# An encoder block on one core: operands, merges, outputs and gates of the attention in pinned pieces, another order at the start of the MLP, the rotary angles later

## The chip, the core and the metric

One core of a Trainium2 chip. The engines that matter: PE (TensorE, the matmuls; PEld are its weight loads), DVE (VectorE), ACT (ScalarE), POOL (GpSimd) and SP (SyncE, which here only issues DMAs). Each runs its own instructions strictly in order and waits for semaphores of the others. The metric is the device time of one execution, in microseconds; "before" is the median of three.

## The reference, cut to what matters

```python
a = rms_norm(h, g_mix[i])
qa, ka, va, qd, kd, vd, gate_na, gate_dil = jnp.split(a @ w_in[i], split_points, axis=-1)
y_na = merge(neighborhood_attention(heads(qa, NA_HEADS), ..., rpb[i]))          # 8 heads of 64
y_dil = merge(dilated_attention(rotary(heads(qd, DIL_HEADS), positions),         # 3 groups x 4 heads,
                                rotary(heads(kd, DIL_HEADS), positions), ...))   # merged by softmax sums
mixed = (jax.nn.sigmoid(gate_na) * (y_na @ w_branch_na[i])
         + jax.nn.sigmoid(gate_dil) * (y_dil @ w_branch_dil[i]))
h = h + mixed @ w_out[i]
c = rms_norm(h, g_mlp[i])
h = h + jnp.square(jax.nn.relu(c @ w_up[i])) @ w_down[i]                         # 1024 -> 4096 -> 1024
e = rms_norm(h, g_ple[i])
h = h + jax.nn.sigmoid(e @ w_ple_gate[i]) * (p[i] @ w_ple_proj[i])
return rms_norm(h, g_final)
```

1024 tokens, 1024 features, one layer, float32 throughout.

## The kernel before

Every float32 operand is split into a high part (a cast, on ACT, line 109) and a low part (the difference, on DVE or POOL, line 110), and each product is three matmuls: high x high, low x high, high x low (lines 208 to 210). So PE needs three passes, and ACT and DVE have a split to make for every operand.

The stages, in us of the profiled execution: v projections (`v_unit`, PSUM tile `ps_v`) and the first RMSNorm to 155; the q and k projections to 375; 12 dilated heads to about 540; 8 NA heads to about 712; the two branch products with the gates (`ps_b`) to 798; `w_out` with the second norm (`ps_t`) to 886; the MLP up (`pp`) to 1205, the MLP down (`ps_d`) to 1510, each by a seven-product scheme on 2 x 2 blocks (b11, b21, b22, t1 to t4, where the t are sums of blocks, made on POOL and DVE); then the input embedding's gate and the final norm.

A scheduler lays out the instructions of each engine from a model of their costs; what is inside `keep_in_program_order` stays, on its engine, in the order of the program. All of a tile's softmax is pinned.

*Attention.* One loop over tiles (128 queries of one head); each step issues the scores of the tile three ahead, the transposes of the present one, its value product two steps later, and matmuls of the gate projection as fill (`pay`). A list `after` holds functions for after a given step, and `later(n, f)` puts f there n steps on. A NA tile: PE scores (`sc`), DVE adds the bias and takes the maximum (`s_sb`, L644, L646), ACT exponential (L647), DVE reciprocal (`rs`, L721), POOL scales (L722), PE transposes (`tp_p`, L731), ACT and DVE split (`pt_h`, `pt_l`), PE values (`av`). The next head's operands (`operands`, L613 to L628) are q scaled and its low half (`q_st`, ACT whole, DVE 64 x 1024) and k and its low part (`k_st`, ACT; `k_lo`, DVE for the NA heads, POOL for the dilated). `dil_merge` and `dil_out` (L937 to L968) weigh the three dilated groups together, each group a whole 128 x 1024 multiply and add (`nm_d`, `fb_d`, `y_d`) on DVE, in the NA heads. Their outputs (`y_raw`, `y_op`) are split after the last head, and the gates (`gt`) are loaded and put through the sigmoid inside the branch loop, at a place that the scheduler chooses.

*Start of the MLP.* `fast_head(u)` loads the first half of block u of `w_up` (`f_raw`) and splits b11 and b21, `fast_sums` loads the second half (`f_raw2`) and makes t1 and t2 on POOL (`f_t`). `norm_to_ops` normalizes a row of tokens, transposes it and makes the sums of the left operand (`s2`, `s3`, `s4`, `keep`). Both share buffers with the `w_out` weights (`ring`, tag `w_raw`).

Of the kernel before, what the change touches and what calls it, by code (L numbers as in the profile page):

```python
# [59 lines left out]
def encoder_kernel(ctx: ExitStack, tc: tile.TileContext, t: dict, out: bass.AP):  # L60
# [236 lines left out]
    with ExitStack() as st:  # L297
# [41 lines left out]

        pi = qp.tile([P, 256], I32, name="pi", tag="rt")  # L340
        for a in range(4):
            nc.sync.dma_start(pi[a * 32:(a + 1) * 32],
                              t["positions"][:, a * 256:(a + 1) * 256].broadcast_to((32, 256)))
        invf = qp.tile([P, 1], F32, name="invf", bufs=1)
        nc.sync.dma_start(invf, t["invf"])
        hpi = qp.tile([P, 1], F32, name="hpi", bufs=1)
        nc.vector.memset(hpi, float(np.pi / 2))
        r, k1, k2, ab, sn, cn = (qp.tile([P, 256], F32, name=n_, tag="rt") for n_ in "abcdef")
        nc.vector.tensor_copy(r, pi)
        nc.vector.tensor_scalar(r, r, invf, None, op0=ALU.mult)  # L350
        big = 4096.0 * TWO_PI
        nc.vector.tensor_scalar(k1, r, 1.0 / big, MAGIC, op0=ALU.mult, op1=ALU.add)
        nc.vector.tensor_scalar(k1, k1, MAGIC, None, op0=ALU.subtract)
        cp = _fixed_parts(big, [2.0 ** (8 - 7 * i) for i in range(8)])
        pp = _fixed_parts(TWO_PI, [2.0 ** (-9 - 12 * i) for i in range(3)])

        def less(k, part, dst=r):
            nc.vector.scalar_tensor_tensor(dst, k, -part, r, op0=ALU.mult, op1=ALU.add)

        for i in range(3):  # L360
            less(k1, cp[i])
        less(k1, cp[3], k2)
        nc.vector.tensor_scalar(k2, k2, 1.0 / TWO_PI, MAGIC, op0=ALU.mult, op1=ALU.add)
        nc.vector.tensor_scalar(k2, k2, MAGIC, None, op0=ALU.subtract)
        less(k2, pp[0])
        less(k1, cp[3])
        less(k2, pp[1])
        less(k1, cp[4])
        less(k1, cp[5])
        less(k2, pp[2])  # L370
        less(k1, cp[6])
        less(k1, cp[7])
        lim = float(np.nextafter(np.float32(np.pi), np.float32(0)))
# [1181 lines left out]
```

## Time and profile before

| what | value |
|---|---|
| median of three executions | 1651.51 us (1649.92 to 1652.97) |
| profiled execution | 1654.93 us, of which the span 1653.1 us |
| mean granted clock of PE | 0.979 |
| PE busy | 1561.5 us, 94% of the span |
| DVE busy | 1193.6 us, 72% |
| ACT, POOL busy | 708.4 us (43%), 652.6 us (39%) |

The span is the time from the first to the last instruction. A clock of 1.00 is 2.4 GHz and a clock of 0.5 is 1.2 GHz, at which each matmul takes twice as long; a mean between them says for what share of a stretch PE ran slow.

### The profile page before, as it was taken

The numbers are of one execution on the slowest core, as the hardware profiler recorded it, in microseconds if no ns is written. First come the engines' busy times: TensorE is split into PE (matmuls) and PEld (weight loads), VectorE is DVE, ScalarE is ACT, GpSimd is POOL, SyncE is SP. The second block draws the span as 40 slices with busy tenths as digits, with TensorE's granted clock in tenths as the row PEclk, the third lists the DMA queues.
The fourth block names the chain that finished last, engine by engine and source line by source line (L and its number), as shares of the span: only waits on it lengthen the run. The fifth ranks groups of instructions, "written<-read, shape, count | busy, mean of one in ns | idle before, by whom it ended". The sixth has DMA issues, their size and how long they took to land. (4 is left out here: it accounts for less than half of the span.)

```text
span 1653.1 us, 22585 instructions
## 1 busy us (share of the span) xinstructions
PE 1561.5 (94%) x7787; PEld 1308.2 (79%) x7787; DVE 1193.6 (72%) x2081; ACT 708.4 (43%) x1327; POOL 652.6 (39%) x434
## 2 busy tenths in 40 slices
PE   8899999999999998889997899999989999999997
PEld 6899777787888877667786688888867788887886
DVE  6744799734666877655458777777778999999855
ACT  7322222226888755654234333333345333323422
POOL 0233578613333222234214677777733322325100
PEclk9999999999999999999998899999999999999999
DMA  8552455675676777655343344444467444434122
GB/s 295 175 152 102 126 167 162 202 259 204 207 215 225 237 240 241 182 179 162 127 166 115 115 140 147 141 147 149 162 234 267 156 163 143 153 102 139 35 101 71
DMA packets 114482, 277.12 MB, mean 168 GB/s; under 512 B 14176, under 2 KB 30528, under 8 KB 113856
## 3 DMA queue, kind: packets, MB, share of 16 engines
q1 hardware_dynamic: 108608, 265.19, 48.9%
q10 hardware_dynamic: 5760, 10.49, 1.7%
q8 instruction: 62, 1.02, 0.2%
q14 instruction: 52, 0.43, 0.1%
HBM read 185.57 MB, written 90.06 MB: 167 GB/s over the span
## 5 line engine op out<-in xcount | busy, mean ns | idle before, releaser
L109 ACT CAST w_hi<-w_raw 128x512 fp32r<-128x512 f32 (+2 forms) x103 | 83.7, 826 | 137.9 <-POOL w_raw L470 56.0
L110 POOL TENSOR_TENSOR w_lo<-w_raw,w_hi 128x512 fp32r<-128x512 f32 (+2 forms) x33 | 64.3, 1951 | 162.0 <-ACT w_hi L109 117.6
L110 DVE TENSOR_TENSOR f_lo<-f_raw,f_hi 128x512 fp32r<-128x512 f32 x80 | 81.6, 1037 | 49.2 <-ACT f_hi L109 48.6
L110 DVE TENSOR_TENSOR w_lo<-w_raw,w_hi 128x1024 fp32r<-128x1024 f32 (+1 forms) x70 | 84.2, 1209 | 36.1 <-ACT w_hi L109 35.8
L722 POOL TENSOR_SCALAR s_sb<-s_sb,rs 128x384 f32<-128x384 f32 x64 | 40.0, 626 | 136.6 <-DVE rs L721 69.1
L110 DVE TENSOR_TENSOR pt_l<-tp_p,pt_h 128x384 fp32r<-128x384 f32 (+3 forms) x120 | 65.1, 542 | 27.0 <-ACT pt_h L109 25.6
L109 ACT CAST f_hi<-f_raw 128x512 fp32r<-128x512 f32 x80 | 46.2, 614 | 79.8 <-DMA f_raw<-w_up 75.7
L109 ACT CAST pt_h<-tp_p 128x384 fp32r<-128x384 f32 (+3 forms) x120 | 56.2, 469 | 33.5 <-PE tp_p L731 27.2
L1178 POOL TENSOR_TENSOR u_t<-u_t 128x512 f32<-128x512 f32 x45 | 53.2, 1183 | 39.9 <-ACT u_t L1177 38.7
L1177 ACT ACTIVATE u_t<-u_t 128x512 f32<-128x512 f32 x45 | 28.4, 631 | 74.5 <-DVE u_t L1164 74.1
L628 POOL TENSOR_TENSOR k_lo<-k_lo,k_st 128x1024 fp32r<-128x1024 f32 x12 | 32.1, 2678 | 65.0 <-ACT k_st L625 47.0
L1341 DVE TENSOR_TENSOR h<-ps_d,h 128x512 f32<-128x512 f32 x84 | 54.7, 681 | 2.4 <-PE ps_d L210 2.2
L110 DVE TENSOR_TENSOR f_lo<-f_t,f_hi 128x512 fp32r<-128x512 f32 x32 | 51.3, 1608 | 1.8
L637 PE MATMUL sc<-k_st,q_st 128*128 128x384 f32 (+3 forms) x160 | 52.3, 327 | 0.2 <-DVE stats L655 0.2
L638 PE MATMUL sc<-k_lo,q_st 128*128 128x384 f32 (+3 forms) x160 | 49.1, 307 | 2.7 <-POOL k_lo L628 2.7
L657 ACT ACTIVATE s_sb<-s_sb,stats 128x256 f32<-128x256 f32 (+2 forms) x96 | 44.9, 469 | 14.9 <-DVE stats L655 14.4
L731 PE MATMUL tp_p<-ident,s_sb 128*128 128x128 f32 x192 | 33.9, 288 | 17.1 <-POOL s_sb L722 15.1
L647 ACT ACTIVATE s_sb<-s_sb,nm 128x384 f32<-128x384 f32 x64 | 39.5, 617 | 23.8 <-DVE nm L646 19.6
L1341 DVE TENSOR_TENSOR sum_t<-ps_d,sum_t 128x512 f32<-128x512 f32 x72 | 46.8, 682 | 2.9 <-PE ps_d L210 2.9
L731 PEld LDWEIGHTS tp_p<-ident,s_sb 128*128 128x128 f32 x192 | 25.1, 147 | 29.9 <-POOL s_sb L722 20.4
L210 PE MATMUL ps_d<-w_hi,m_op 128*128 128x512 f32 x112 | 44.3, 405 | 2.6 <-DVE m_op L110 2.6
L644 DVE CUSTOM_DVE_ANT_0 s_sb<-bias,sc 128x384 f32<-128x384 f32 x64 | 35.1, 548 | 15.8 <-PE sc L638 14.1
(482 smaller groups left out, 5809.1 us busy)
## 6 DMA issues: line engine op xcount, KB each, us to landing
f_raw<-w_up SPq DMA_DIRECT2D x32, 512.0 KB
w_raw<-w_in SPq DMA_DIRECT2D x26, 512.0 KB
u_raw<-l_scr SPq DMA_DIRECT2D x25, 512.0 KB
qk_scr<-o SPq DMA_DIRECT2D x96, 128.0 KB
h<-l_scr SPq DMA_DIRECT2D x24, 512.0 KB
l_scr<-u_t SPq DMA_DIRECT2D x42, 256.0 KB
l_scr<-u_s SPq DMA_DIRECT2D x42, 256.0 KB
w_raw<-w_qk SPq DMA_DIRECT2D x20, 512.0 KB
```

Of the source, the lines that this page charges most:

```text
L109: nc.scalar.copy(hi, src)
L110: eng.tensor_tensor(lo, src, hi.bitcast(F32), op=ALU.subtract)
L210: nc.tensor.matmul(ps, sl, mh, start=False, stop=last)
L637: pe(nc.tensor.matmul(o, qs[:, qsl], kk, start=True, stop=False))
L638: pe(nc.tensor.matmul(o, qs[:, qsl], ll, start=False, stop=True))
L644: nc.vector.tensor_tensor_reduce(s_[:, :n], bias, sc[:, :n], 1.0, -3.0e38, op0=ALU.subtract, op1=ALU.max, accum_out=mx)
L647: nc.scalar.activation(s_[:, :n], s_[:, :n], AF.Exp, bias=nm, scale=1.0, accum_out=sm)
L657: nc.scalar.activation(s_[:, :n], s_[:, :n], AF.Exp, bias=nm, scale=-1.0, accum_out=sm)
L722: nc.gpsimd.tensor_scalar(pr, pr, rs, 1.0, op0=ALU.mult, op1=ALU.mult)
L731: pe(nc.tensor.transpose(tp[:, i * P:(i + 1) * P], pr[:, kb * P:(kb + 1) * P], ident))
L1178: nc.gpsimd.tensor_tensor(c, c, c, op=ALU.mult)
L1341: nc.vector.tensor_tensor(d, ps, d, op=ALU.add)
```

## The change

Eight edits, none of which changes what is computed or the number of matmuls:

1. The rotary angles (24 DVE operations, two sines on ACT, their DMAs) move from before the v products to after the second v unit.
2. `operands(h)` returns four steps, spread with `later` over four tiles: q's low half in two 64 x 512 pieces and, for NA heads, k's low part in two 128 x 512 pieces, all pinned; for NA heads from the fourth tile after the raw load, for dilated heads from the third tile of the head before.
3. `dil_merge` runs after NA tile 6, `dil_out` after 22 and 38, and its multiplies and adds are halves, 3, 4 and 5 tiles after the loads instead of 5 and 6.
4. Outputs 4 and 5 are split inside the last NA head, the other four after it, all in pinned halves.
5. The gates are loaded and put through the sigmoid in program order, three ahead of their use.
6. `w_out` ends with the half rows (6,0), (7,0), (6,1), (7,1); the heads of MLP blocks 0 and 1 come before (6,1); the norms of rows 6 and 7 follow with high priority; the last row's `keep` and block 0's second half use spare `ring` tiles; the first four MLP products are b11 of blocks 0 and 1, then b21 of both.
7. The first chunk of the MLP down runs b11, b21, b22, t1 ... instead of the order in `DOWN`; the second half of the last chunk's `u_scr` loads into a free operand tile (`u_more`) after b11 of that chunk.
8. The last tile's gate product is cut 384 + 128 instead of 256 + 256 columns.

```diff
         s1 = []
         for u in range(5):
             v_unit(u)
+            if u == 1:
+                angles()
...
+            def q_low(c):
+                keep(nc.vector.scalar_tensor_tensor(qs[b, c], q_raw[b, c], -0.125, qs[b, c].bitcast(F32),
+                                                    op0=ALU.mult, op1=ALU.subtract))
+            def step_0():
+                keep(nc.scalar.activation(qs, q_raw, AF.Copy, scale=-0.125))
+                q_low(cols[0])
+            def step_1():
+                keep(nc.scalar.copy(ks, kf))
+                q_low(cols[1])
...
-            if cb == 2 and qt == 1 and h < 7:
-                ready_ops.append(operands(h + 1))
             if qt == 0:
                 na_loads(*((h, cb + 1) if cb < 3 else (h + 1, 0)))
+            elif cb == 0 and h < 7:
+                load_raw(h + 1)
+                for n, f in enumerate(operands(h + 1)):
+                    later(3 + n, f)
...
-            later(5, scaled)
-            later(6, added)
+            later(3, lambda: scaled(0))
+            later(4, lambda: (scaled(1), added(0)))
+            later(5, lambda: added(1))
...
+        for n, f in ((50, lambda: y_load(4, "bias", 3)), (53, lambda: y_split(4, "kl", 3)), (54, lambda: y_load(0, "md", 2)),
+                     (55, lambda: y_load(1, "md", 2)), (56, lambda: y_split(5, "st", 4)), (57, lambda: y_load(2, "bias", 3))):
+            after.setdefault(na_0 + n, []).append(f)
...
+            load_row(NT - 1)
+            half_row(NT - 1, 0)
+            heads = [fast_head(u) for u in range(2)]
...
+            half_row(NT - 2, 1)
+            with tc.high_priority(offset=150):
+                norm_to_ops(np_, op_, *before.pop())
+                half_row(NT - 1, 1)
+                norm_to_ops(np_, op_, *before.pop())
+            late = fast_sums(0, heads[0], spare[1], op_.tile([P, D], F32, name="f_t", tag="keep"))
...
+                if u == 0:
+                    p1[0], p1[1] = head_1(0), head_1(1)
+                    for v in range(2):
+                        head_2(v, p1[v])
                 fast_rest(heads[u], *late)
...
+        first_order = ("b11", "b21", "b22", "t1", "t2", "t3", "t4")
...
+                if o == "b11":
+                    u_more = m_ops[0].bitcast(F32).rearrange("p (f n) -> p f n", f=2)
+                    nc.sync.dma_start(u_more, u_scr[2:4].rearrange("f p n -> p f n"))
```

How the order of the engines moves, at three places. DVE in an NA head, where the next head's operands meet the second `fb_d` of a dilated output; before:

```order
L964 TENSOR_TENSOR fb_d<-nm_d,fb_d 128x1024
L721 RECIPROCAL rs<-sm 128x1
L110 TENSOR_TENSOR pt_l<-tp_p,pt_h 128x3x128
L644 ISA s_sb,mx<-bias,sc 128x384
L644 ISA mx 128x1
L627 SCALAR_TENSOR_TENSOR q_st<-q_raw,q_st 64x1024
L644 ISA s_sb,mx<-bias,sc 128x384
L644 ISA mx 128x1
L628 TENSOR_TENSOR k_lo<-k_lo,k_st 128x1024
L110 TENSOR_TENSOR pt_l<-tp_p,pt_h 128x3x128
L646 TENSOR_SCALAR nm<-mx 128x1
L968 TENSOR_TENSOR y_d<-y_d,fb_d 128x1024
```

and of the change, the same operands and the first half of the same `fb_d`:

```order
L633 SCALAR_TENSOR_TENSOR q_st<-q_raw,q_st 64x512 x2
L674 TENSOR_SCALAR nm<-mx 128x1
L637 TENSOR_TENSOR k_lo<-k_lo,k_st 128x512
L110 TENSOR_TENSOR pt_l<-tp_p,pt_h 128x3x128
L749 RECIPROCAL rs<-sm 128x1
L110 TENSOR_TENSOR pt_l<-tp_p,pt_h 128x3x128
L672 ISA s_sb,mx<-bias,sc 128x384
L672 ISA mx 128x1
L749 RECIPROCAL rs<-sm 128x1
L674 TENSOR_SCALAR nm<-mx 128x1
L637 TENSOR_TENSOR k_lo<-k_lo,k_st 128x512
L1003 TENSOR_TENSOR fb_d<-nm_d,fb_d 128x512
```

Four whole operations stood within twelve rows; now the pieces are halves with the softmax of other tiles between them.

ACT at the end of the last NA head, before (`gt` is the sigmoid of a gate, `s_sb` a tile's exponential):

```order
L1058 ACT_TABLE_LOAD
L1058 ACTIVATE gt<-gt 128x1024
L109 CAST pt_h<-tp_p 128x3x128
L647 ACT_TABLE_LOAD
L647 ACTIVATE s_sb,sm<-s_sb,nm 128x384
L762 COPY fold<-av 64x512
```

and of the change, after the last tile:

```order
L1073 CAST y_op<-y_raw 128x512 x6
L1073 CAST y_op<-y_na 128x512 x2
L1110 ACT_TABLE_LOAD
L1110 ACTIVATE gt<-gt 128x1024 x4
```

Sigmoids no longer stand between the exponentials, and there is one table load where there were five.

POOL at the start of the MLP, before (`f_raw_9112` is block 0's second half, `f_raw_9379` block 1's; `keep` and `s4l` with `s_9172` are row 7's sums):

```order
L186 TENSOR_TENSOR f_t<-f_raw_9112,f_raw 128x512
L186 TENSOR_TENSOR f_t<-f_raw_9379,f_raw 128x512
L187 TENSOR_TENSOR f_t<-f_raw_9112,f_t 128x512
L188 TENSOR_TENSOR f_raw_9112<-f_raw_9112 128x512
L187 TENSOR_TENSOR f_t<-f_raw_9379,f_t 128x512
L188 TENSOR_TENSOR f_raw_9379<-f_raw_9379 128x512
L189 TENSOR_TENSOR f_raw<-f_raw,f_t 128x512 x2
L1118 TENSOR_TENSOR keep<-keep,s_9172 128x512
```

and of the change (`f_raw_9428` is block 1's second half, `w_lo` block 0's, `keep` and `w_hi` the sums of rows 6 and 7, `s4l` a low part of each):

```order
L189 TENSOR_TENSOR f_raw<-f_raw,f_t 128x512
L1184 TENSOR_TENSOR keep<-keep,s_9138 128x512
L1185 TENSOR_TENSOR keep<-keep,hx 128x512
L110 TENSOR_TENSOR s4l<-keep,s4h 128x512
L1184 TENSOR_TENSOR w_hi<-w_hi,s_9209 128x512
L1185 TENSOR_TENSOR w_hi<-w_hi,hx 128x512
L186 TENSOR_TENSOR f_t<-w_lo,f_raw 128x512
L110 TENSOR_TENSOR s4l<-w_hi,s4h 128x512
```

Block 0's first sum (t1) stood ahead of the last row's sums; now it stands behind five operations for rows 6 and 7.

## Rows read from the trace of the kernel before

**Rows 1.** The page, its first part: busy time of each engine with its share of the span and its instructions.

```profile
PE 1561.5 (94%) x7787; PEld 1308.2 (79%) x7787; DVE 1193.6 (72%) x2081; ACT 708.4 (43%) x1327; POOL 652.6 (39%) x434
```

**Rows 2.** Stretches of the run (from:to in us): length, then busy time (and instructions) of PE, PEld, DVE, ACT and POOL, the granted clock of PE as a share of full speed, the DMA share and GB/s.

```profile
50.00:75.00 25.00, 19.64 (x141) 18.97 (x140) 16.93 (x42) 7.10 (x11) 2.61 (x2) 0.86 0.41 113
75.00:150.00 75.00, 75.00 (x628) 75.00 (x627) 40.42 (x46) 20.21 (x32) 31.36 (x19) 1.00 0.50 155
...
375.00:575.00 200.00, 194.33 (x1186) 164.87 (x1185) 132.66 (x411) 159.14 (x400) 63.01 (x40) 1.00 0.66 213
575.00:700.00 125.00, 108.46 (x601) 92.59 (x600) 90.71 (x261) 75.09 (x166) 28.44 (x43) 0.92 0.72 226
700.00:725.00 25.00, 19.72 (x98) 14.89 (x96) 14.87 (x21) 17.77 (x23) 5.59 (x5) 1.00 0.63 194
725.00:800.00 75.00, 69.82 (x296) 56.41 (x297) 39.27 (x52) 31.99 (x40) 34.66 (x22) 0.98 0.49 156
...
875.00:950.00 75.00, 57.40 (x227) 45.00 (x226) 60.55 (x78) 30.37 (x57) 44.95 (x31) 0.86 0.34 113
...
1200.00:1300.00 100.00, 91.46 (x373) 72.03 (x372) 82.56 (x84) 47.51 (x58) 36.09 (x15) 0.95 0.63 227
...
1475.00:1525.00 50.00, 46.20 (x200) 37.53 (x199) 48.17 (x71) 13.49 (x24) 30.70 (x18) 0.97 0.30 105
```

**Rows 3.** From 30 to 70 us: the first transposes of PE after its longest stop there (start, length, operation, idle time before with its releaser); the angles' line 358 (length, DVE busy and instructions, clock, DMA share, GB/s); another of their lines as a group (count, busy us, mean ns, idle before).

```profile
58.94 1.12 PE L275 MATMUL tp<-ident,xn 128*128 128x128 f32 x4 [5.31 <-DVE act10l L110]
...
30.00:70.00 40.00, 4.96 (x12) 0.91 0.52 162
...
L349 DVE CAST a<-pi 128x256 f32<-128x256 int32 x1 | 0.3, 295 | 1.0 <-DMA pi<-positions 1.0
```

**Rows 4.** What PE waited for from 375 to 575 us: line, releaser, us in total, times, longest.

```profile
PE sc L638 <- POOL k_lo L628: 2.7, 3, 1.2
```

**Rows 5.** What PE waited for from 575 to 700 us (the same columns); then in order of time one of these stops: DVE from 640 to 648 us and PE at its end.

```profile
PE tp_p L731 <- POOL s_sb L722: 14.6, 6, 4.4
...
640.03 2.02 DVE L964 TENSOR_TENSOR fb_d<-nm_d,fb_d 128x1024 f32<-128x1024 f32 x1
...
643.07 1.22 DVE L627 SCALAR_TENSOR_TENSOR q_st<-q_raw,q_st 64x1024 fp32r<-64x1024 f32 x1
...
644.80 1.22 DVE L628 TENSOR_TENSOR k_lo<-k_lo,k_st 128x1024 fp32r<-128x1024 f32 x1
...
646.47 1.21 DVE L968 TENSOR_TENSOR y_d<-y_d,fb_d 128x1024 f32<-128x1024 f32 x1
...
649.56 0.90 PE L731 MATMUL tp_p<-ident,s_sb 128*128 128x128 f32 x3 [4.35 <-POOL s_sb L722]
```

**Rows 6.** Loads of the NA stretch: the issue of a `q_raw` on SP and its first use on ACT, and the issue of the two `fb_d` whose first use is the DVE row at 640.03 above. No use has an idle mark, so none waited.

```profile
561.57 0.33 SPq L613 DMA_DIRECT2D q_raw<-qk_scr  x1
...
574.83 1.07 ACT L624 ACTIVATE q_st<-q_raw 128x1024 fp32r<-128x1024 f32 x1
...
628.98 1.14 SPq L960 DMA_DIRECT2D fb_d<-f_scr  x2
```

**Rows 7.** What PE waited for from 700 to 725 and from 725 to 800 us, and one of ACT's five table loads in the last NA head.

```profile
PE ps_b L208 <- ACT y_op L109: 1.5, 1, 1.5
...
PE ps_b L208 <- DVE gt L1064: 3.0, 2, 1.8
...
700.38 1.28 ACT L1058 ACT_TABLE_LOAD   x1
```

**Rows 8.** The start of the MLP: two of w_out's matmuls on PE (24 starts apart), what PE waited for from 875 to 950 us, SP's load of the first w_up block, and rows of DVE and POOL.

```profile
879.67 0.39 PE L210 MATMUL ps_t<-w_hi,act11l 128*128 128x512 f32 x1
...
885.11 0.39 PE L210 MATMUL ps_t<-w_hi,act11l 128*128 128x512 f32 x1
...
PE pp L208 <- ACT f_hi L109: 8.2, 1, 8.2
PE pp L208 <- ACT act10h L109: 5.0, 1, 5.0
...
884.80 0.33 SPq L183 DMA_DIRECT2D f_raw<-w_up  x1
...
907.39 5.15 DVE L110 TENSOR_TENSOR f_lo<-f_t,f_hi 128x512 fp32r<-128x512 f32 x3
...
914.87 0.68 DVE L110 TENSOR_TENSOR f_lo<-f_raw,f_hi 128x512 fp32r<-128x512 f32 x1
...
908.57 3.42 POOL L189 TENSOR_TENSOR f_raw<-f_raw,f_t 128x512 f32<-128x512 f32 x2
918.32 1.28 POOL L1118 TENSOR_TENSOR keep<-keep,s 128x512 f32<-128x512 f32 x1 [6.33 <-DVE s L1115]
919.56 1.73 POOL L1119 TENSOR_TENSOR keep<-keep,xn 128x512 f32<-128x512 f32 x1
```

**Rows 9.** What PE waited for from 1200 to 1300 us.

```profile
PE ps_d L210 <- DVE m_op L110: 2.6, 1, 2.6
```

**Rows 10.** Around 1500 us: SP's second load into u_raw, one of DVE's four splits of it, and PE.

```profile
1488.24 0.38 SPq L1380 DMA_DIRECT2D u_raw<-u_scr  x1
...
1496.85 1.77 DVE L110 TENSOR_TENSOR act00l<-u_raw,act00h 128x512 fp32r<-128x512 f32 x1
...
1504.42 0.47 PE L208 MATMUL ps_d<-w_hi,act00h 128*128 128x512 f32 x1 [3.48 <-DVE h L1341]
```

More of the change, by code (lines that the diff above doesn't have):

```diff
@@ L337, in encoder_kernel @@
             norm_to_act(qp, two(xs[tt]), g, tt, xn=qp.tile([P, D], F32, name="xn", tag="nat"))
[L340 to L373, printed above, removed]
-        nc.vector.tensor_scalar(r, r, lim, -lim, op0=ALU.min, op1=ALU.max)
-        nc.vector.scalar_tensor_tensor(ab, r, -1.0, r, op0=ALU.mult, op1=ALU.max)
-        nc.scalar.activation(sn, r, AF.Sin)
-        nc.scalar.activation(cn, ab, AF.Sin, bias=hpi, scale=-1.0)
-        for i, src in enumerate((cn, sn)):
-            nc.sync.dma_start(cs_scr[i].rearrange("a f n -> (a f) n"), src)
         def v_unit(u):
@@ L833, in dil_score @@
                     dil_v(g_, pr_, pair, 0)
+            if qi == 2:
+                for n, f in enumerate(operands(h + 1 if h < 19 else 0)):
+                    later(1 + n, f)
             if qi == 4:
-                ready_ops.append(operands(h + 1 if h < 19 else 0))
                 if h < 19:
@@ L999, in encoder_kernel @@
         nc.sync.dma_start(blk, t["blk"])
-        ready_ops.append(operands(8))
+        for f in operands(8):
+            f()
         early[0] = True
@@ L1128, in encoder_kernel, with half_row @@
             w8 = take(8, 0)
-            before = None
-            for tt in range(NT):
+            sums, before = {}, []
+            def half_row(tt, n):
+                hx, parts = sums[tt]
+                ps = tok_product(w8, tt, n)
+                c = slice(n * HALF, (n + 1) * HALF)
+                nc.vector.tensor_tensor(hx[:, c], ps, hx[:, c], op=ALU.add)
+                parts.append(square_part(np_, hx[:, c], ps))
+                if n == 1:
+                    nc.sync.dma_start(h_scr[tt * P:(tt + 1) * P, :], hx)
+                    before.append((hx, g, tt, parts))
@@ L1131, in encoder_kernel, with load_row @@
+            def load_row(tt):
                 hx = op_.tile([P, D], F32, name="hx", tag="hx", bufs=2)
                 nc.sync.dma_start(hx, t["x"][tt * P:(tt + 1) * P, :])
-                parts = []
+                sums[tt] = (hx, [])
+            for tt in range(NT - 2):
+                load_row(tt)
                 for n in range(2):
-                    ps = tok_product(w8, tt, n)
-                    c = slice(n * HALF, (n + 1) * HALF)
-                    nc.vector.tensor_tensor(hx[:, c], ps, hx[:, c], op=ALU.add)
-                    parts.append(square_part(np_, hx[:, c], ps))
-                    if before is not None and n == 0:
-                        norm_to_ops(np_, op_, *before)
-                    if tt == NT - 1 and n == 0:
-                        heads = [fast_head(u) for u in range(2)]
-                        late = fast_sums(0, heads[0], op_.tile([P, D], F32, name="f_raw2", tag="hx", bufs=2),
-                                         op_.tile([P, D], F32, name="f_t", tag="keep"))
@@ L1282, in encoder_kernel @@
         ops, lefts, raws = {}, {}, {}
+        first_order = ("b11", "b21", "b22", "t1", "t2", "t3", "t4")
+        seq = [(0, o) for o in first_order] + [(c, o) for c in range(1, 7) for o in DOWN]
         def load_left(n):
@@ L1351, in encoder_kernel @@
                 load_left(n)
-            for o in DOWN:
+            for o in first_order:
                 operands(0, o)
```

185 lines of the change are left out of this document (130 added, 55 removed).

## The prediction

> **What bounds the kernel now.** I read the page's busy times first. PE is busy 1561.5 of 1653.1 us [rows 1], the other engines far less, and the change leaves PE's matmuls as many as they were. So it can only give back time in which PE stood or ran below full speed. The second view cuts the run into stretches [rows 2]. In each, the loss is (length − PE busy) + (1 − clock) × length; the second term is right because at the lower level, 1.2 GHz, half of the time is lost, and the mean clock falls by the same half. This gives for 50–75 us 5.4 + 3.5 = 8.9; 375–575 (dilated heads) 5.7; 575–700 (NA heads) 16.5 + 10.0 = 26.5; 700–725 5.3; 725–800 (branch products) 5.2 + 1.5 = 6.7; 875–950 (start of the MLP) 17.6 + 10.5 = 28.1; 1200–1300 (start of the MLP down) 8.5 + 5.0 = 13.5; 1475–1525 3.8 + 1.5 = 5.3. Together 100 us: that is all that these edits can reach. The third view is what PE waited for in each stretch, and the fourth the rows just ahead of such a stop.
>
> **The change part by part.**
>
> *Angles.* From 30 to 70 us DVE spends 4.96 us on line 358 [rows 3] and about 2.4 on eight more operations of their kind, of which the cast of 0.30 us is one; 7.4 us in all, between the norms whose transposes PE waits for. PE's longest stop there is 5.31 us, for DVE's split of a transposed tile [rows 3], and the slow clock after it costs 3.5. At the new place, after the second v unit, DVE is busy 40 of 75 us and PE never stands [rows 2], so the operations are covered; without that cover they would cost their 7.4. Nothing needs the tables before q and k. Bounds 0 and −8.9; most of the 7.4 us stands ahead of the stop, so I take −7.
>
> *Dilated operands.* PE waits 2.7 us for `k_lo` from POOL [rows 4]; the rest of the 5.7 is spread thin. The operands start two tiles earlier, which covers `k_lo`. Bounds 0 and −5.7; I take −3.
>
> *NA operands, merge and dilated outputs.* PE waits 14.6 us, in six stops, for POOL's scaled probabilities [rows 5], though POOL is busy 28 of 125 us. The rows ahead of the stop of 4.35 us show why: from 640 to 648 us DVE runs 2.02 + 1.22 + 1.22 + 1.21 = 5.7 us of other work, and the maxima and reciprocals that POOL needs are queued behind it. That work comes to halves, a tile apart, so no more than about 1.3 us (two halves) should stand together where 2 did, and the operands no longer fall on the outputs' `y_d`. But the work itself stays: DVE is busy 90.7 us here, and eight output pieces come in, each about 0.68 us [rows 8], 5.4 in all: 96. Were the whole loss to go, 98.5 us would be left and DVE 98% full, which an engine that works in order beside two others will not reach. With 12 us back it is 96 of 113, 85%, about what stretches without stops bear. Bounds −4 (one long stop goes) and −22; I take −12.
>
> *Outputs and gates.* After the last tile PE waits for `y_op`, and later for `gt` [rows 7]; these two stretches lose 12.0. Two of six outputs are ready by then. Sigmoids no longer stand between exponentials: five ACT table loads of 1.28 us [rows 7] become one, 5.1 us less on ACT in the last head. Gates loaded three ahead take away ACT's waits for them. The first branch product still has to wait for four outputs split in a row. Bounds −3 and −11; I take −8.
>
> *Start of the MLP.* The `w_up` load leaves SP at 884.80 [rows 8] and the last product of `w_out` ends at 885.5, so PE waits 8.2 us for the cast of it, then 5.0 for transposed tokens. Now the heads load before the last half rows, so the first stop shrinks to an estimated 1.5 us. Four products follow, 48 matmuls at (885.11 − 879.67)/24 = 0.227 us [rows 8], 10.9 us. Then t1 is wanted. Its first sum now stands in POOL's queue behind five operations for rows 6 and 7, each 1.28 to 1.73 us [rows 8], 7.5 in all; these start when row 7's sums leave DVE, by my estimate 10 us after the end of `w_out` (the transposes, two copies, three adds). So t1 comes 10 + 7.5 + 1.3 + a cast and a split of 1.3 = 20 us after, and PE has run dry at 1.5 + 10.9 = 12.4: a new stop of 7 to 9 us. Of the 17.6 us of standing about 11 remain, and of the slow clock its share, 11/17.6 × 10.5 = 6.5, and 1.5 for the rest: 19 of 28.1. I take −9; bounds +5 (the queue of loads on SP is late too) and −20 (the sums keep up).
>
> The row that speaks against this part: three DVE splits took 5.15 us, 1.7 each, while POOL ran its own sums (3.42 us for two), and 0.68 us once POOL had stopped [rows 8]. The Trainium skill (GPSIMD Engine Reference, section 8, Key points) says that POOL shares its SBUF interfaces with DVE and contends with DVE instructions that have two SBUF inputs; the trace agrees, with 1.7 against 0.68 us. By that rule the six DVE operations ahead of t1 would take 6 us longer and the term would be −3.
>
> *MLP down.* The stop of 2.6 us for the low part of `m_op` [rows 9] and those after it come from operands made by DVE out of the last up blocks; the new order asks for the same cast and load in its third product. I take 0; bounds +4 and −4.
>
> *Second half of `u_scr`.* Its load leaves SP at 1488.24, and its splits fall among DVE's last evacuations, one at 1496.85 taking 1.77 us; PE then stops 3.48 us at 1504 for DVE's `h` [rows 10]. Loaded early, the splits stand among the earlier sums. Bounds 0 and −5.3; I take −4.
>
> *Last tile.* The same columns in two other pieces: 0, ± 0.5.
>
> Sum: −7 − 3 − 12 − 8 − 9 + 0 − 4 = −43. The profiled execution took 1654.93 us, 1.8 more than its span and 3.4 more than the median; from it 1611.9, from the median 1651.51 − 43 = 1608.5.
>
> **The rivals.**
>
> *DVE is the bound of the NA heads.* The clumps are smaller, but the work is the same plus 5.4, and two `y_na` folds, a q half and a `y_d` half can still stand in a row. For it: DVE is over 80% busy wherever PE stops long. Against: 575–700 has 34 us of idle DVE. Then NA gives nothing and the outputs 4 instead of 8: 43 − 16 = 27, 1624.5.
>
> *The start of the MLP keeps its loss,* as t1 comes later by POOL and the port: term 0, 43 − 9 = 34, 1617.5.
>
> *Slower: pinned operations wait for their loads.* ACT's scaling of q is now pinned three tiles after its load, and each dilated output's multiply three tiles instead of five after `fb_d`. A tile takes (712 − 540)/64 = 2.7 us, three 8.1. Before, 13.3 us lay between the load and the cast of `q_raw`, and 11.0 for `fb_d` [rows 6], so landings after 8.1 us would not have shown. Seven casts and six multiplies stand ahead of the softmax in their queues. If the loads take all that time, the waits are 7 × 5.2 + 6 × 2.9 = 54 us, and 1651.5 − 43 + 54 = 1662; it decides from 43/13 = 3.3 us each, landings at 11.4 us. Against: the 1 MB of a head's q and k needs 4.6 us at the 226 GB/s of this stretch [rows 2].
>
> *No effect:* the stops come back elsewhere as the next tile's, within 3 us of 1651.5.
>
> **How the numbers follow.** Chances: forecast 0.57 (its own range 1599 to 1617), DVE bound 0.17, MLP start 0.13, no effect 0.05, slower 0.08. The predicted time is 1608.5. Below, the bounds of NA and MLP start together (−10, −11) would reach 1588, but hardly both: 1593. Above, both first rivals at once give 1633.5, which I take as 1634. A measurement of this kernel tells about 0.2%, 3.3 us, from no change. Faster 0.87, same 0.05, slower 0.08.
>
> **What would show it.** Right: in 50–75 us PE's stop for DVE under 1 us; in the NA heads stops for POOL's `s_sb` under 8 us together; one table load after the last head; at the start of the MLP one long stop, before t1, with POOL's sums as its cause; no stop at 1504. Wrong: ACT or DVE idle for `q_raw` or `fb_d` in the heads; DVE over 95% busy there with PE still stopping; a first MLP stop as long as before.

## The result and the profile after

The changed kernel takes **1623.33 us** (median of four, 1622.1 to 1625.92) against 1652.24 for the kernel before beside it; the ratio is 0.9825 with a 95% interval of 0.9807 to 0.9843, so 26 to 32 us less. The forecast was 1608.5, in a range of 1593 to 1634: faster as forecast, by 29 us instead of 43. The profiled execution took 1623.57 us, its span 1621.8.

The first part of the page after, to be read beside [rows 1]:

```profile
PE 1544.0 (95%) x7787; PEld 1294.8 (80%) x7787; DVE 1200.7 (74%) x2125; ACT 700.8 (43%) x1329; POOL 658.0 (41%) x434
```

The same stretches as in [rows 2] (length, busy time of PE, PEld, DVE, ACT and POOL, granted clock, DMA share, GB/s). Stages come 8 us earlier at 375 us and 31 at the end, so the stretches hold somewhat later work than before.

```profile
50.00:75.00 25.00, 24.47 (x207) 24.27 (x206) 19.64 (x26) 8.62 (x14) 10.55 (x7) 1.00 0.73 211
375.00:575.00 200.00, 193.38 (x1198) 165.21 (x1197) 142.13 (x458) 159.15 (x407) 59.53 (x43) 1.00 0.67 214
575.00:700.00 125.00, 114.40 (x656) 96.16 (x655) 98.01 (x278) 81.22 (x177) 37.62 (x44) 0.99 0.77 251
875.00:950.00 75.00, 63.05 (x264) 50.66 (x265) 57.85 (x64) 29.49 (x53) 54.95 (x38) 0.91 0.31 102
1200.00:1300.00 100.00, 93.35 (x397) 75.79 (x396) 97.83 (x95) 48.16 (x55) 33.92 (x12) 0.97 0.65 224
```

PE's waits after (line, releaser, us in total, times, longest), from 50 to 75, 375 to 575, 540 to 700, 685 to 800, 840 to 950, 1185 to 1300 and 1450 to 1500 us, a "..." between two stretches:

```profile
PE tp L275 <- DVE ny L248: 0.5, 1, 0.5
...
PE tp_p L890 <- DVE pt_l L110: 2.8, 3, 1.4
...
PE tp_p L759 <- POOL s_sb L750: 6.3, 8, 1.4
PE tp_p L759 <- DVE pt_l L110: 2.4, 2, 1.3
...
PE ps_b L208 <- DVE gt L1127: 3.9, 3, 1.6
PE ps_b L208 <- ACT y_op L1073: 2.3, 1, 2.3
...
PE pp L208 <- ACT f_hi L109: 12.2, 2, 11.0
...
PE ps_d L210 <- DVE m_op L110: 4.6, 2, 3.4
PE ps_d L208 <- ACT act11h L109: 3.6, 1, 3.6
...
PE ps_d L208 <- DVE sum_t L1436: 1.5, 2, 1.1
PE ps_d L208 <- DVE h L1436: 1.0, 1, 1.0
```

What the reader is to see: the 5.31 us stop at 59 us is gone; the stops for `s_sb` are no fewer than before, but short; at the start of the MLP one stop of 11 us stands in the place of two of 8 and 5; and in the place of the stop of 3.48 us at 1504 there are three of 0.3 to 1.1 us.

To compare stages that have moved I counted, for each, the time between starts of PE's matmuls beyond the usual time of their form (it holds stops and slow clock together); this is what a stage "lost". To 75 us it fell from 13.9 to 5.8; in the q and k projections it was 8.8 and 9.3; from the first score to the first branch product 43.4 and 23.7; in the branch products 10.1 and 9.4; from there to the first MLP product 10.2 and 1.8; in the next 168 matmuls of the MLP up 17.4 and 19.8; in the rest of the MLP up **−0.1 and 6.9**; in the first 84 matmuls of the MLP down 11.2 and 13.2, in the others 10.1 and 4.0. Together −31 us, as the two spans say. The 6.9 us in the middle of the MLP up are what the prediction did not have at all.

The changed kernel starts its branch products ahead of the last tile's value products, so the attention is best read between matmuls that both kernels have in the same number. From the first score to the first value product of the NA heads it takes 154.0 us before and 153.2 after; from there to the value products of the last six tiles 164.7 and 148.9; and from there to the first matmul of `w_out` 90.3 and 86.5. The second of these stretches, before and after:

```profile
537.82:702.48 164.66, 147.75 (x837) 126.61 (x837) 121.66 (x362) 104.07 (x230) 38.25 (x59) 0.94 0.71 224
...
528.79:677.68 148.89, 140.00 (x836) 119.56 (x836) 127.27 (x390) 99.80 (x230) 44.70 (x60) 1.00 0.80 256
```

### The profile page after: what moved, and what is told of

Read it like the earlier page. It is cut to its first block, busy times and chain, and to the rows that moved or that the text cites. A ratio compares the mean times of both kernels' runs of the same rounds, so it can differ in the third digit from the quotient of the medians.

```text
span 1621.8 us, 22641 instructions
## 1 busy us (share of the span) xinstructions
PE 1544.0 (95%) x7787; PEld 1294.8 (80%) x7787; DVE 1200.7 (74%) x2125; ACT 700.8 (43%) x1329; POOL 658.0 (41%) x434
## 5 line engine op out<-in xcount | busy, mean ns | idle before, releaser
L750 POOL TENSOR_SCALAR s_sb<-s_sb,rs 128x384 f32<-128x384 f32 x64 | 46.3, 724 | 112.6 <-DVE rs L749 65.3
L109 ACT CAST pt_h<-tp_p 128x384 fp32r<-128x384 f32 (+3 forms) x120 | 55.7, 468 | 26.2 <-PE tp_p L759 21.3
L685 ACT ACTIVATE s_sb<-s_sb,stats 128x256 f32<-128x256 f32 (+2 forms) x96 | 44.9, 469 | 14.8 <-DVE stats L683 13.9
L210 PE MATMUL ps_d<-w_hi,m_op 128*128 128x512 f32 x112 | 42.9, 391 | 4.6 <-DVE m_op L110 4.6
L499 POOL TENSOR_TENSOR o<-x,c 128x512 f32<-128x512 f32 x24 | 40.6, 1707 | 11.2 <-DVE c L494 8.7
L208 PE MATMUL ps_b<-y_op,w_hi 128*128 128x512 f32 x96 | 38.3, 401 | 6.3 <-DVE gt L1127 3.9
L208 PE MATMUL ps_d<-w_hi,m_op 128*128 128x512 f32 x112 | 43.6, 390 | 0.0
```

The costliest lines, as they stand in the source:

```text
L109: nc.scalar.copy(hi, src)
L208: nc.tensor.matmul(ps, sh, mh, start=first, stop=False)
L210: nc.tensor.matmul(ps, sl, mh, start=False, stop=last)
L499: nc.gpsimd.tensor_tensor(dst, x, y, op=op)
L685: nc.scalar.activation(s_[:, :n], s_[:, :n], AF.Exp, bias=nm, scale=-1.0, accum_out=sm)
L750: nc.gpsimd.tensor_scalar(pr, pr, rs, 1.0, op0=ALU.mult, op1=ALU.mult)
```

## The experiments

All times are medians beside runs of the kernel before on the same chip; what counts is the ratio to these. In us of 1651.5, the changed kernel has −28.9.

### Each part alone

The first three put one group of edits into the kernel before, the fourth takes one out of the changed kernel.

`e1_angles`, edit 1 alone:

```diff
+            if u == 1:
+                angles()
```

> The kernel before with edit 1 alone (the angles after the second v unit). Theory: the stop of 5.31 us before the transposes at 59 us and the slow clock behind it go, the rest of the run is as before: 1651.5 - 8 = about 1644 (the first 75 us lost 13.9 us before and 5.8 us in the changed kernel). Rival: the time won is given back at the next shared limit, within 3 us of 1651.5.

Measured 1644.49 us, ratio 0.9945 (0.9928 to 0.9962): −9.1. The first 75 us lost 5.8 as in the changed kernel, and nothing was given back. The forecast's −7 had the right place and was 2 short by the median, though inside the interval (−6.3 to −11.9); the first theory holds.

`e2_attention`, edits 2 to 5 alone:

```diff
+                for n, f in enumerate(operands(h + 1)):
+                    later(3 + n, f)
...
+            later(3, lambda: scaled(0))
...
+        for k, tag, bufs in ((0, "v_t", 3), (1, "st", 4), (2, "pt_h", 2), (3, "pt_l", 2)):
+            y_split(k, tag, bufs)
...
+        for n in range(3):
+            gate_in(n)
```

> The kernel before with edits 2 to 5 alone (operands, merge, outputs, gates). By the two traces this part, from 375 to 800 us, lost about 19 us less in the changed kernel: 1651.5 - 19 = about 1632. By the terms of the prediction (-3, -12, -8) it is -23, 1628. Rival, that these edits also cost the new stops of PE in the middle of the MLP (950 to 1200 us, 5.7 us): then those stops appear here too, and the time is about 1638.

Measured 1631.94 us, ratio 0.9884 (0.9852 to 0.9917): −19.2. From the first score to the first branch product it lost 23.4 us (43.4 before), and in the middle of the MLP up 0.8: the new stops are not this part's.

`e3_mlp_start`, edit 6 alone:

```diff
+            heads = [fast_head(u) for u in range(2)]
...
+            half_row(NT - 2, 1)
+            with tc.high_priority(offset=150):
+                norm_to_ops(np_, op_, *before.pop())
+                half_row(NT - 1, 1)
+                norm_to_ops(np_, op_, *before.pop())
...
+                if u == 0:
+                    p1[0], p1[1] = head_1(0), head_1(1)
```

> The kernel before with edit 6 alone (another order at the start of the MLP). By the two traces the start (875 to 950 us) lost 5 us less in the changed kernel, but the middle of the MLP up (950 to 1200 us) 5.7 us more. Theory A, the new stops in the middle belong to this edit: PE stops for DVE's part sums between 950 and 1200 us come to 4 us or more here and the time is within 3 us of 1651.5. Theory B, they do not: no such stops, 1651.5 - 5 = about 1646.5. The prediction's term was -9, 1642.5.

Measured 1653.92 us, ratio 1.0007 (0.9994 to 1.002): nothing. PE's waits from 945 to 1195 us, of this kernel; the kernel before has none there:

```profile
PE pp L208 <- DVE part L1189: 4.2, 7, 1.4
```

Theory A holds. The way into the MLP and its first 168 matmuls lost 21.3 us here and 27.6 before, and the matmuls after these 6.8 against −0.1: what the start wins, the middle gives back.

`e4_without_7`, the changed kernel without edit 7:

```diff
-        first_order = ("b11", "b21", "b22", "t1", "t2", "t3", "t4")
...
-                    u_more = m_ops[0].bitcast(F32).rearrange("p (f n) -> p f n", f=2)
-                    nc.sync.dma_start(u_more, u_scr[2:4].rearrange("f p n -> p f n"))
```

> The changed kernel without edit 7 (the first chunk of the MLP down in its old order, the second half of the last chunk's u_scr loaded late). By the two traces the two parts gave 1.6 and 2.5 us: 1623.3 + 4 = about 1627.5, with PE's stop of 3.5 us near the end of the MLP down back. Rival, either stop is only moved to the next thing that PE waits for: 1623 to 1625. The prediction's terms (0 and -4) also give 1627.

Measured 1625.32 us, ratio 0.9835 (0.9809 to 0.986): edit 7 is worth some 2 us, less than the two intervals resolve, and the time lies between the theory's and the rival's. The profiles say more: after the first 84 matmuls the MLP down lost 8.0 us here and 4.0 with the edit; in the kernels with it 3.4 to 5.5, in those without it 7.7 to 10.3, but for `e11` below (5.4). In the first 84 matmuls 11.5 and 13.2, in all kernels 10.2 to 13.2 with no order in it. Where the 4 us lie tells on: only about 1 of them is in the last 252 matmuls, where `u_more` is used, since three short stops stand in the place of the long one. About 3 are in matmuls 169 to 252, the second chunk's first, where PE's stop of 1.7 us for DVE's `h` is gone; these kernels lost 3.7 us there without edit 7 and 0.8 with it (0.1 to 1.2 in all kernels with it, 1.4 to 4.3 in those without). That is just behind the chunk whose order was changed, but the two halves of edit 7 were not run apart.

The parts add up: −9.1 − 19.2 + 1.2 − 1.7 = −28.8, where all together gave −28.9. Each has an interval of 4 to 11 us from end to end, so that they agree this closely is chance. Edit 8 was not run alone; behind the MLP down PE lost 0.8 us before and 0.7 after.

### Why the start of the MLP gives nothing

The rows of the changed kernel around one of the new stops, roughly in order of time: POOL's first sum of a block, DVE's splits of its t1 and t2, PE's use of a t4, ACT's outputs and casts, DVE's split of the next t4, SP's loads of two halves of blocks of `w_up`, then ACT, DVE and PE (start, length, operation, idle time before and its releaser):

```profile
1112.22 1.29 POOL L186 TENSOR_TENSOR f_t<-f_raw,f_raw 128x512 f32<-128x512 f32 x1 [3.00 <-DMA f_raw<-w_up]
...
1115.68 3.48 DVE L110 TENSOR_TENSOR f_lo<-f_t,f_hi 128x512 fp32r<-128x512 f32 x2
...
1116.34 0.39 PE L210 MATMUL pp<-act11h,f_lo 128*128 128x512 f32 x1
...
1121.84 0.63 ACT L1265 ACTIVATE u_t<-u_t 128x512 f32<-128x512 f32 x1 [4.27 <-DVE u_t L1252]
...
1123.94 0.60 ACT L109 CAST f_hi<-f_raw 128x512 fp32r<-128x512 f32 x1
...
1124.77 0.33 SPq L183 DMA_DIRECT2D f_raw<-w_up  x1
...
1125.26 0.93 DVE L110 TENSOR_TENSOR f_lo<-f_raw,f_hi 128x512 fp32r<-128x512 f32 x1
...
1126.21 0.33 SPq L177 DMA_DIRECT2D f_raw<-w_up  x1
...
1132.83 1.14 ACT L109 CAST f_hi<-f_raw 128x512 fp32r<-128x512 f32 x2 [6.36 <-DMA f_raw<-w_up]
...
1133.49 1.33 DVE L110 TENSOR_TENSOR f_lo<-f_raw,f_hi 128x512 fp32r<-128x512 f32 x1 [3.77 <-ACT f_hi L109]
...
1136.44 3.47 DVE L110 TENSOR_TENSOR f_lo<-f_t,f_hi 128x512 fp32r<-128x512 f32 x2
1139.83 0.68 DVE L1252 TENSOR_TENSOR part<-pp,p 128x512 f32<-128x512 f32 x1
...
1140.66 0.47 PE L208 MATMUL pp<-act01h,f_hi 128*128 128x512 f32 x1 [1.43 <-DVE part L1252]
```

The load at 1126.21 is late for ACT by 6.36 us, ACT for DVE by 3.77, and the evacuation of a product (`part`) stands in DVE's queue behind the splits that waited, so PE waits for a PSUM buffer. And the load itself is late since it waits for its place: the raw tile of a block holds b11 and b21, t4 is summed into b21's place, and the load leaves as soon as DVE has split that t4 (at 1126.19).

The cast ahead of this split (the one at 1123.94) can only come once PE is done with t4 of the block before, whose operand has a single buffer (`fast_split(fp, "g", 1, ...)`). In the kernel before, in blocks 2 to 4, it came within 0.9 us of that. Here it is not what holds the cast: PE was done with that t4 at 1116.73, and in blocks 3 to 13 the cast came 6.5 to 8.2 us after PE was done. Ahead of it in ACT's queue stand outputs (`u_t`), which waited 4.27 us for DVE's evacuations, and these stood behind DVE's splits of t1 and t2 of the next block, whose sums POOL, idle for 3.00 us, could only start when that block's second half had landed. That half in turn had waited for the splits of the block before it to free its place. So the loads, POOL, ACT and DVE form a ring, and PE is held by it where it waits for a PSUM buffer.

Counted from the starts of PE's matmuls, a block (seven products of 12, 84 matmuls) took 19.04 us all through the middle of the kernel before and 19.04 to 20.8 in the changed one. The loads show how much room each had: before, block 2's first half left SP at 917.52, and PE's first product of it began at 937.47 (20.0 us); in the changed kernel 895.49 and 902.48 (7.0), and 9.3 to 10.1 from the next block on, which is as near as the ring lets PE come. In the kernel before this distance shrank block by block and reached 10.1 only at the end of the MLP up. `e3` shows it with nothing else changed: block 2's first half left at 920.42 and PE began at 927.40, so PE came 10.1 us sooner than before and the load 2.9 us later, and from block 4 on the distance stays at 10.1 to 10.3.

`e5_t4_away` opens the ring:

```diff
-        t1, t2 = t12[:, 0:HALF], t12[:, HALF:]
+        t1, t2, t4 = b11, t12[:, 0:HALF], t12[:, HALF:]
...
-        nc.gpsimd.tensor_tensor(b21, b21, t2, op=ALU.subtract)
+        nc.gpsimd.tensor_tensor(t4, b21, t2, op=ALU.subtract)
```

> The changed kernel with one edit in the MLP up: block u's first sum t1 takes the place of b11 and t4 goes to the freed half of f_t instead of the place of b21, so that the raw tile of a block is free once t1 is split, and not only after t4 is (t4's operand has one buffer, which PE holds until the block before is done). Theory: from its second block on, PE runs in a loop with the load of w_up (PE's t4, ACT's cast and DVE's split of the next t4, the load, its cast and split, PE), 19.2 to 20.7 us a block where its matmuls need 19.04; with the tile free earlier the loop is open, all blocks take 19.0 to 19.1 us, PE's stops for DVE's part sums between 945 and 1195 us (4.4 us) go, and the time is 1623.3 - 5 = about 1618. Rival, the stops come from DVE's own load of work, not from the loads: blocks stay at 19.2 to 20.7 us, 1623 +- 2.

Measured 1616.64 us, ratio 0.9786 (0.9771 to 0.98): 6.4 us below the changed kernel. The stretch from 950 to 1150 us (columns as above) of the kernel before:

```profile
950.00:1150.00 200.00, 200.00 (x883) 165.44 (x882) 142.74 (x164) 68.73 (x121) 147.73 (x103) 1.00 0.42 145
```

of the changed kernel:

```profile
950.00:1150.00 200.00, 196.63 (x859) 160.29 (x858) 141.97 (x164) 69.41 (x122) 148.16 (x103) 1.00 0.44 150
```

and of this one:

```profile
950.00:1150.00 200.00, 200.00 (x884) 165.63 (x883) 149.38 (x169) 72.89 (x125) 142.15 (x105) 1.00 0.46 154
```

ACT's wait for the loads in that stretch, in the changed kernel:

```profile
ACT f_hi L109 <- DMA f_raw<-w_up: 52.1, 10, 6.4
```

and in this one:

```profile
ACT f_hi L109 <- POOL f_raw L186: 51.8, 11, 4.9
...
ACT f_hi L109 <- DMA f_raw<-w_up: 13.3, 10, 2.2
```

All blocks after the first take 19.04 us, PE never stands, though DVE does more work in the stretch than in the changed kernel: the rival (DVE's own load) falls. Block 2's first half now leaves SP at 874.15, not at 895.49, and from there on 30 to 31 us ahead of its use. ACT still waits, now for POOL's first sum, but PE no longer pays for it.

Two things stay open. The 6.4 us are not all the ring's: against the changed kernel's profile the middle of the MLP up lost 7.3 us less, but its first 168 matmuls 3.7 more, and 2.9 less were lost in the first 84 matmuls of the MLP down, where the kernels differ by as much without an order. And the edit does more than free the tile: the two halves that leave SP 1.2 to 1.8 us apart in the changed kernel now leave 3.7 us and more apart, and from the issue of a second half to POOL's first sum of it 3.9 to 4.4 us pass from block 3 on, where it was 6.6 to 8.2. Which of the two opened the ring was not run apart.

`e6_without_6`, the changed kernel with the start of the MLP as before:

```diff
-            half_row(NT - 2, 1)
-            with tc.high_priority(offset=150):
-                norm_to_ops(np_, op_, *before.pop())
-                half_row(NT - 1, 1)
-                norm_to_ops(np_, op_, *before.pop())
+            norm_to_ops(np_, op_, *before)
```

> The changed kernel with the start of the MLP in its old order (without edit 6). By the loop theory that edit only moves PE nearer to the loads: without it the start loses 5 us more, but the blocks after it take 19.04 us each, and the time is within 3 us of 1623.3. Rival, in the changed kernel the edit is worth its 5 us: about 1628.

Measured 1623.67 us, ratio 0.9825 (0.9803 to 0.9846), the same as with the edit. Blocks 2 to 10 take 19.04 us, and only then come stops for `part` (2.4 us in three): here PE reaches the ring at the end.

`e11_t4_away_on_before`, the edit of `e5` in the kernel before:

```diff
-        nc.gpsimd.tensor_tensor(b21, b21, t2, op=ALU.subtract)
+        nc.gpsimd.tensor_tensor(t4, b21, t2, op=ALU.subtract)
```

> The kernel before with the one edit of the MLP up that took 6.7 us off the changed kernel (t1 in the place of b11, t4 in f_t). Theory: in the kernel before PE starts later against the loads, never comes up to them (each block takes 19.04 us), and the edit gives nothing: 1651.5 to 1654, within 0.2% of before. Rival, the edit helps by itself (the split of t4, the norms or the first blocks): 1645 to 1648.

Measured 1643.23 us, ratio 0.995 (0.9933 to 0.9967): −8.3, the rival's direction and somewhat more than its time, and my expectation fell. The part of it that I had reasons for holds, since in the middle of the MLP up nothing changed (19.04 us a block with and without). The gain stands at both ends. PE's waits from 840 to 945 us, in this kernel:

```profile
PE pp L208 <- ACT f_hi L109: 7.8, 1, 7.8
PE pp L208 <- ACT act10h L109: 5.8, 1, 5.8
PE tp L275 <- DVE xn L258: 1.4, 1, 1.4
PE pp L209 <- DVE s2l L110: 0.9, 1, 0.9
```

The stop for a low part of the sums, 2.9 us (`s3l`) in the kernel before, is 0.9 (`s2l`), and the first 168 matmuls lose 13.9 us instead of 17.4. Of the rest, the MLP down lost 5.4 us after its first 84 matmuls, where the kernels with the same code there lose 7.7 to 10.3; one trace does not tell why.

### What holds t1, the operands, the halves, the gates

`e7_t1_early`, t1 of block 0 on POOL ahead of the sums of rows 6 and 7 and in the place of b11; besides, DVE's part of the two norms is pinned ahead of the splits of `w_up`:

```diff
             half_row(NT - 2, 1)
             with tc.high_priority(offset=150):
+                nc.gpsimd.tensor_tensor(b11, b12, b11, op=ALU.subtract)
                 norm_to_ops(np_, op_, *before.pop())
...
+                if i == 0 and tt == NT - 1:
+                    early_sums()
```

> The changed kernel with block 0's first sum t1 made on POOL before the sums of rows 6 and 7 (in the place of b11), DVE's part of the two norms pinned ahead of the splits of w_up, and t1 split right behind row 7's transposed tokens. Theory, POOL's queue holds t1: PE's stop of 11.0 us before t1 shrinks to about 6 us (row 7's first operand is split at about 880 us), a second one of about 4 comes before t2, whose sum still waits behind the rows' sums, and the time is 0 to 3 us lower. Rival, the norm of row 7 or the load holds t1: the stop stays at about 11 us.

Measured 1621.01 us, ratio 0.9812 (0.9797 to 0.9826): 2 us less, though the intervals meet. The changed kernel's POOL, PE and DVE:

```profile
874.15 1.27 POOL L1184 TENSOR_TENSOR keep<-keep,s 128x512 f32<-128x512 f32 x1 [5.79 <-DVE s L1181]
...
881.60 1.71 POOL L1185 TENSOR_TENSOR w_hi<-w_hi,hx 128x512 f32<-128x512 f32 x1
883.27 1.25 POOL L186 TENSOR_TENSOR f_t<-w_lo,f_raw 128x512 f32<-128x512 f32 x1
...
885.23 0.80 PE L208 MATMUL pp<-act10h,f_hi 128*128 128x512 f32 x1 [11.01 <-ACT f_hi L109]
...
885.21 6.64 DVE L110 TENSOR_TENSOR f_lo<-f_t,f_hi 128x512 fp32r<-128x512 f32 x4
891.78 0.68 DVE L110 TENSOR_TENSOR f_lo<-w_lo,f_hi 128x512 fp32r<-128x512 f32 x1
```

and PE in this kernel:

```profile
876.79 0.79 PE L213 MATMUL pp<-act10h,f_hi 128*128 128x512 f32 x1 [2.39 <-ACT act10h L114]
880.93 0.80 PE L214 MATMUL pp<-act10l,f_hi 128*128 128x512 f32 x1 [3.35 <-DVE act10l L115]
882.61 0.80 PE L215 MATMUL pp<-act10h,f_lo 128*128 128x512 f32 x1 [0.89 <-DVE f_lo L115]
888.28 0.50 PE L215 MATMUL pp<-s2h,f_lo 128*128 128x512 f32 x1 [0.86 <-DVE f_lo L115]
```

POOL's queue did hold t1: it stood idle for 5.79 us, its sums of rows 6 and 7 came first, and t1 at 883.27. With t1 early PE's first product of it starts 8.4 us sooner (the stage itself 1.7), but then row 7's own tokens and DVE's splits bind it, 7.5 us in four stops. The first 168 matmuls lose 18.6 us, only 1.2 less.

`e9_operands`, edit 2 alone in the kernel before:

```diff
+            if qi == 2:
+                for n, f in enumerate(operands(h + 1 if h < 19 else 0)):
+                    later(1 + n, f)
```

> The kernel before with edit 2 alone (the next head's operands in pinned pieces, at other tiles). By the two traces the dilated heads lost 1 us less in the changed kernel; of the NA heads' gain I give the operands a third, 5 us: 1651.5 - 6 = about 1645.5, with PE's waits for k_lo gone and those for s_sb (14.6 us before) at about 10. Rival, the merge alone makes the clumps: 1650, with waits of 13 us or more for s_sb.

Measured 1644.16 us, ratio 0.9953 (0.9937 to 0.9969): −7.8. PE's waits, two from 375 to 575 us and, behind the second "...", two from 540 to 700:

```profile
PE tp_p L887 <- DVE pt_l L110: 2.8, 3, 1.4
...
PE sc L663 <- POOL k_lo L648: 0.2, 1, 0.2
...
PE tp_p L756 <- POOL s_sb L747: 8.5, 5, 3.7
PE tp_p L756 <- DVE pt_l L110: 4.2, 2, 2.5
```

The waits for `k_lo` went from 2.7 [rows 4] to 0.2, and PE waits 2.8 us for `pt_l` instead, each time two tiles earlier: the dilated heads gain nothing (154.3 us for 154.0). The gain is in the NA heads (155.6 for 164.7); of their long stops one of 3.7 us is left, at 685 us, and ahead of it DVE runs a whole `fb_d` multiply (1.98 us) and `y_d` addition (1.21) of the merge.

`e8_whole`, the places of the changed kernel, but whole operations for the operands' low parts and the dilated outputs' multiplies and adds:

```diff
-            cols = [slice(0, HALF), slice(HALF, S)]
+            cols = [None, slice(0, S)]
...
-                c = slice(i * HALF, (i + 1) * HALF)
+                if i == 0:
+                    return
+                c = slice(0, S)
```

> The changed kernel with the operands' low parts and the dilated outputs' multiplies and adds whole again instead of in halves, each whole at the step of its second half; the places of the changed kernel stay. If cutting in halves is what shortens the waits of the NA heads: DVE's 64 x 1024 and 128 x 1024 operations take 1.2 to 2.0 us at one go again, PE's waits for POOL's scaled probabilities rise from 6.3 us (8 stops) to 12 or more, and the time is 1628 to 1635. If the places do it: waits of 6 to 8 us and 1623 to 1625.

Measured 1626.35 us, ratio 0.9845 (0.983 to 0.9859), 3 us above the changed kernel, with intervals that meet. From 540 to 712 us:

```profile
PE tp_p L763 <- POOL s_sb L754: 6.4, 6, 1.6
...
PE tp_p L763 <- DVE pt_l L110: 2.1, 2, 1.1
```

6.4 us for `s_sb`, as with halves (6.3): that the four operations no longer stand within twelve rows gives the gain. In the NA heads cutting them adds nothing (148.4 us whole, 148.9 in halves); the 3 us by which the profile is slower in the attention lie in the dilated heads (156.1 for 153.2).

`e10_gates_free`, the changed kernel without edit 5:

```diff
-        for n in range(3):
-            gate_in(n)
...
+                nc.sync.dma_start(gt, g_scr.rearrange("(b f) p n -> f p b n", b=2)[f, :, :, c])
+                nc.scalar.activation(gt, gt, AF.Sigmoid)
```

> The changed kernel without edit 5 (each gate is loaded where it is used and its sigmoid placed by the scheduler). One sigmoid stands between exponentials of the last head again, three ACT table loads of 1.28 us where there is one. Theory: the loads and the waits of ACT for the gates cost PE 2 to 4 us between 690 and 800 us, 1623.3 + 3 = about 1626. Rival, ACT has room for them: within 1 us of 1623.3.

Measured 1621.45 us, ratio 0.9819 (0.9799 to 0.9838): no loss. With the table loads back PE has a stop of 1.6 us for ACT's `pt_h` in the last head again (1.8 in the kernel before, none in the changed one), but from the first branch product to the first matmul of `w_out` both kernels, with the same matmuls, take 83.1 to 83.2 us. The rival holds.

### Both findings together

`e12_both` joins the early t1 and, from block 1 on, the tile of `e5`:

```diff
+                nc.gpsimd.tensor_tensor(b11, b12, b11, op=ALU.subtract)
...
-        nc.gpsimd.tensor_tensor(b21, b21, t2, op=ALU.subtract)
+        nc.gpsimd.tensor_tensor(t4, b21, t2, op=ALU.subtract)
```

> The changed kernel with t1 of block 0 made early on POOL and with the raw tile of w_up freed early in all blocks from the second on. Theory, the two add: the first 84 products take 38.4 us as with the early t1 alone (40.3 in the changed kernel), the blocks after them 19.04 us each: 1623.3 - 1.9 - 5 = about 1616 at most, and 1611 if the start is also as much earlier than with the freed tile alone (44.3 us there) as these two differ. Rival, the order that the scheduler finds puts one of the two stops back: 1616.5 to 1621.

Measured **1614.5 us**, ratio 0.9783 (0.9761 to 0.9804), the lowest median of all and by the ratio 6.9 below the changed kernel's, though not to be told from `e5`'s. It meets the theory's "at most 1616", but not by blocks of 19.04 us alone: from block 3 on every block takes that; the two before it take 20.5 and 20.6, since block 0's raw tile is held here until its t4 is split, and block 2's first half, which takes its place, leaves SP at 894.44. Since edit 6 was worth nothing with the ring closed, and the first products of `e5` lose more (23.5 us) than those of `e11` (13.9, after 7.4 more on the way to them), it may be worth nothing with the ring open as well: the changed kernel without edit 6 and with the tile of `e5` was not run.

## Why the prediction was right, and where it was not

**Angles, −7:** right in place, −9.1 measured, about 8 by the traces. The stop went whole (0.5 us for `ny` is left) and the slow clock with it, so the bound of −8.9 was nearer than −7.

**Dilated operands, −3:** too much. `k_lo`'s 2.7 us were taken as the loss, but when that wait went, one of 2.8 us for `pt_l` came two tiles ahead of the same three places. The stretch of the dilated heads shrank by 0.8 us.

**NA heads, −12:** right in mechanism, short in size. Between the same matmuls 15.8 us went (164.7 to 148.9), of which the operands alone took 9.0 (`e9`) and the merge and the outputs, moved apart from them, the rest. The limit that the term was taken from holds: DVE is now busy 127.3 of 148.9 us, the 85% of the sum. What came back more than I gave is the clock, 0.94 before and 1.00 after, beside stops of at most 1.4 us.

**Outputs and gates, −8:** oversized. From the last six tiles to `w_out` 3.8 us went; waits of 3.9 and 2.3 us are left there. The table loads went as told, and `e10` shows them worth nothing. The errors of these three terms cancel: the sum of the attention was −23, −20.4 by the traces and −19.2 measured. That is luck.

**Start of the MLP, −9:** the step that failed. Its first half is as put: the first stop shrank to 1.5 us, with 1.2 for the next cast, and one stop before t1 came in, with POOL's sums as its cause, 11 us where 7 to 9 were estimated. But the sum ended at the stage's own end. It took for granted that PE, once earlier, stays earlier, and never asked how far ahead of PE the loads of `w_up` ran in the 300 us behind: from 20 us down to 10 in the kernel before, by the loads above, so all of that room was spoken for. `e3` and `e6` put the whole edit at 0, and `e5`, where the loads leave earlier and the blocks take 19.04 us, shows why. The rival of this step had the size (term 0, 1617.5) by another mechanism: t1 did come later by POOL, but the start even so lost 6.0 us less (27.6 to 21.6), and the 7.0 more in the middle took that back. A misreading besides: the load at 884.80 in [rows 8] is that of block 0's second half; the first half, which PE waited for, left SP at 886.24.

The Trainium skill (GPSIMD Engine Reference, section 8, Key points) says that POOL shares its SBUF interfaces with DVE and contends with DVE instructions that have two SBUF inputs; the prediction weighed that at 6 us. The trace after agrees with it again: DVE's four splits of block 0 beside POOL's sums took 6.64 us, 1.66 each, and 0.68 alone. With t1 out of POOL's way (`e7`) these splits are among what PE waits for next.

**MLP down 0, `u_more` −4:** right in sum by the profiles (means over the kernels with and without: 11.7 against 11.4 us in the first 84 matmuls, 4.4 against 8.3 in the others), though the times alone give −1.7. The split is wrong: `u_more` gave about 1 us, since in the place of the stop at 1504 PE has three short ones, and about 3 came in matmuls 169 to 252, behind the reordered chunk, for which the sum had 0.

**The rivals.** DVE as the bound fell: at 98 of 125 us, 78%, PE's waits were short. The slower one came in a trace of its form only: DVE waited 2.3 us for `fb_d`, in two waits, and ACT never for `q_raw`. The DVE rival's number, 1624.5, is the nearest of all to the 1623.33 measured, and that is chance, since the NA heads gave more than the forecast and not nothing. By the runs of the parts, the sum is −28.8 in the place of −43: −9.1 for −7, −19.2 for −23, +1.2 for −9, −1.7 for −4. So the faster time came from angles and attention as told, and the time lies in the stated range, but above the forecast's own (1599 to 1617), for the most part by the start of the MLP.

## What to carry to other kernels

Ahead of a gain at the start of a long steady stage, count in the trace how far that stage's loads run ahead of their use at its first and last block: where the distance shrinks to a floor, the stage is a ring through its buffers, and what is won ahead of it is given back. To open such a ring, look for the tile that is held longest for the least (here a sum written back into the loaded tile) and put that result somewhere else. And when a short wait is taken away, look for the wait that comes next to the same place; where long stops slowed the clock, ask whether the stops left are short enough to keep it, as its share may come back whole.

## What the runs showed of the hardware

A load of 512 KB that follows another of 512 KB by 1.2 to 1.8 us took 5.0 to 6.6 us from its issue to the cast that waited for it, a spread of 1.6 us between blocks of the same code, and the one ahead of it 6.6 to 8.2 us to its first use; where the two were 3.7 us and more apart (`e5`), ACT waited 2.2 us at most, and the other's first use came after 3.9 to 4.4 us. And in the NA heads, between the same matmuls, eight stops of 1.4 us and less for `s_sb` stand beside a granted clock of 1.00, where seven of up to 4.4 us stood beside 0.94 (between the levels of 2.4 and 1.2 GHz).
